# Half of the gates and branches by rows of tokens in a DeepNorm decoder trunk on one Trainium2 core

## The chip, the cores and the metric

The kernel runs on one core of a Trainium2 chip. The metric is the device time of one execution in microseconds (us), smaller is better. The core has five engines with a queue of instructions each: TensorE (PE; its weight loads are shown apart as PEld), VectorE (DVE), ScalarE (ACT), GpSimd (POOL) and SyncE (SP), which here does nothing but issue transfers. A queue is worked off in order: an instruction that waits holds up everything behind it on its engine.

## The reference

A decoder trunk of two layers over 256 tokens of width 1024, all in float32. Each layer is a half-step SwiGLU block, a mixer, and a second half-step SwiGLU block, each followed by a scaled residual and a layer norm. The change is in the mixer:

```python
    z = x @ w_in
    u, v, q, k, val, gates = jnp.split(z, SPLITS, axis=-1)
    ...
    h_a = _chunked_sgu(u, v, sgu_ln_g, sgu_ln_b, sgu_w, sgu_b)
    ...
    o = _diff_attention(q, k, val, lam_full)
    o = _rmsnorm(o, diff_ln_g) * (1.0 - lam_init)
    h_b = o.reshape(bsz, seq, DIFF_V_WIDTH)
    g = jax.nn.sigmoid(gates.reshape(bsz, seq, N_BRANCH, D_MODEL) + gate_b)
    m = g[:, :, 0] * (h_a @ w_branch[0]) + g[:, :, 1] * (h_b @ w_branch[1])
    return m @ w_out
```

So there are two gates of 1024 columns, each a product of the 256 x 1024 input with a 1024 x 1024 matrix and a bias; two branches, each again a product with a 1024 x 1024 matrix; the gated sum m; and the product of m with `w_out`.

## The kernel before, in words

**Numbers in two parts.** Every matrix product is made from float32 numbers split in a high part and a low remainder, both in a rounded float32 type. A product takes three passes: high by high, low weight by high input, high weight by low input. The weights come from memory as float32 and are split on the chip: `stream` (L150) issues a 1 MB load on SP into one of 4 `raw` buffers, ACT copies the high part into `whi` (L169) and DVE subtracts to give `wlo` (L171). One load gives two *pieces* of 128 x 1024 weights, and there are 8 buffers each for high and low pieces. An input in two parts lies with 256 high and 256 low values side by side, so that one matmul of 512 columns takes both.

**By columns of features.** `gemm_a2` (L243) holds a 128 x 128 block of weights in the array and streams tokens past it. For a block of 128 features it makes 8 wide matmuls of 512 columns (high weight by both parts of the input, L253) and 8 narrow ones of 256 columns (low weight by the high part, L260). The result stands with features on the partitions. It is evicted by ACT (one half, L261) and DVE (which adds the other, L263), four times for 512 features. The gates, `u`, `q`, `k` and both branches are made so.

**By rows of tokens.** `gemm_b` (L282) and `gemm_b2` (L302) hold a 128 x 128 block of the input (128 tokens) and stream 512 columns of weights; `rows_b` (L272) and `three` (L238) make three wide matmuls (L241) for each of the 8 values of k (blocks of 128 input features). The token halves t = 0 and t = 1 come one after the other. In `gemm_b` the last `tail` values of k are held back: their weights are used for all of t = 0 and then again for t = 1. In `gemm_b2`, which makes 1024 columns from two matrices of 512, all weights are. The result stands with tokens on the partitions, and one instruction evicts 512 columns.

**Order.** PE's order is written out in the code. Work that runs beside the big products is a generator handed to `beside` with a delay; `beat` counts PE's work in units and lets due generators emit their next instructions. A block of 128 features by columns counts 0.65 and 0.35, a piece of one token half by rows 0.5. The order on the other engines is made by the compiler's scheduler from priorities (program order) and readiness, and `behind(ins)` puts an instruction behind a given one of the same engine: `emptied` and `added` are the last eviction on ACT and DVE, `loaded` the last weight load on SP.

**A mixer's stages.** `val` (rows), then 8 times `q` or `k` (columns), each attended by a task beside; then gate A and gate B (columns, L727 to L736), `u` in part, `v` (rows), the rest of `u`, branch B from `hb` (the attention's output), branch A from `ha` (the spatial unit's output), the gated sum, and `w_out` (rows, L825). A branch (L804) is two calls of `gemm_a2` with two loads each; DVE multiplies a result with the gate (L808), and for branch A adds branch B's part (L815) and splits the sum into `mhi` and `mlo` (L206, L207), which stand with features on the partitions, as `w_out` needs them. In `w_out` the first half of k comes first for both token halves. Then comes the layer norm, whose result for t = 0 is turned by PE (L507) while t = 1 is still being made, and the next SwiGLU block, whose first weights are split into buffers that `w_out` gives back.

**Turning by transfer.** The SwiGLU block makes most of its hidden values by rows, and has to turn them: `parted` (L184) copies the 16-bit halves of the float32 numbers into two planes on POOL, `moved` (L188) is a transposing transfer on SP, `joined` (L192) puts the halves together again, and ACT and DVE split the result (L554, L556). This is the existing use of what the change does to the gated sum.

Of the kernel before, what the change touches and what calls it, by code (L numbers as in the profile page):

```python
# [20 lines left out]
P = 128  # L21
# [17 lines left out]
NEG = -1e30  # L39
ROPE_THETA = 10000.0  # L40
# [13 lines left out]
def trunk(ctx, tc, x, xT, w13a, w13b, w2, wb, wqk, wa, wbr, wo, gateb, sgug, sgub, sguwT, sgubias, lam, diffg,  # L54
# [247 lines left out]
    def gemm_b2(srcs, xh, xl, done, norm=None):  # L302
# [9 lines left out]
        for t in range(NT):  # L312
            for c in range(2):
                if norm:
                    norm.ready(t, c)
                    after[3] = [norm.xlo.get((0, 1))] * 2
                for m in range(2):
                    n = 2 * c + m
                    if t == 0:
                        got[m][2 * c : 2 * c + 2] = stream(srcs[m][:, c * CH : (c + 1) * CH], sub=512, lent=lent[n],  # L320
                                                           after=after[n])
                    for i in range(2 * c, 2 * c + 2):
                        rows_b(ps[t][m], t, 2 * i, got[m][i], xh, xl, KT)
            with behind(latest[0] if t == 0 else None):
                done(t, ps[t])
# [255 lines left out]
    def mixer(l, i, norm):  # L581
        xh, xl = parts(both)
        V_, VAL_ = 0, 1
        U_, GA_, GB_ = 0, 1, 2
# [137 lines left out]
        for hp in range(HEADS // 2):  # L722
            qT = rope(wqk[l, hp, 0], HD ** -0.5)
            kT = rope(wqk[l, hp, 1], 1.0)
            beside(attend(hp, qT, kT), 4.5 + 2.1 * hp)

        gates = []  # L727
        for br, sec in ((0, GA_), (1, GB_)):
            gt = slots("gate", KT)
            gates.append(gt)  # L730
            for c in range(KT // 2):
                (_, b), = gemm_a2([wa[l, sec, c]], both, lambda m: t512("gz"), lambda: t512("r"))
                for n in range(2):
                    s = slice(n * T, (n + 1) * T)
                    A.activation(gt[c][:, s], b[:, s], AF.Tanh, scale=0.5,
                                 bias=gbh[:, l, br, c * 2 + n : c * 2 + n + 1])  # L736
# [4 lines left out]
        def u_part(gps):  # L741
            for gp in gps:
                uu = slots("u", 2)[0]
                us.append(uu)
                (_, uu), = gemm_a2([wa[l, U_, gp]], both, lambda m: uu)
# [58 lines left out]
        def branch(br, h):  # L804
            for c in range(0, KT // 2, 2):
                for m, b in gemm_a2([wbr[l, br, c + m] for m in range(2)], lambda k: h[k], lambda m: t512("bz")):
                    g = gates[br][c + m]
                    V.scalar_tensor_tensor(out=g, in0=g, scalar=1.0, in1=b, op0=ALU.add, op1=ALU.mult)  # L808
                    yield c + m, g

        for _ in branch(1, hb):
# [13 lines left out]
        gemm_b2([wo[l, 0], wo[l, 1]], view(m_hi), view(m_lo), done)  # L825
# [3 lines left out]
    for l in range(DEPTH):  # L829
# [5 lines left out]
_INS = ["x", "xT", "w13a", "w13b", "w2", "wb", "wqk", "wa", "wbr", "wo", "gateb", "sgug", "sgub", "sguwT", "sgubias",  # L835
        "lam", "diffg", "lng", "lnb", "lngT", "lnbT", "cosT", "sinT"]


def _layout(i):
# [39 lines left out]
    o["wa"] = np.stack([pairs(w) for w in (u, ga, gb)], axis=1)  # L879
    o["wbr"] = pairs(f["w_branch"])  # L880
# [35 lines left out]
```

## Time and profile before

| | |
|---|---|
| median of 3 runs | 1220.32 us (1219.88 to 1220.91) |
| the profiled execution's own time | 1220.37 us |
| its span, first to last instruction | 1218.6 us |
| granted TensorE clock | 1.0 |

The profile is of one execution. The span is 1.8 us shorter than the time of the same execution, since the time holds what lies around the instructions. Times in the trace count from the span's start. A row of the chain of work gives the start, the duration, the engine with tile and line, and how many instructions were merged. A row of a group of instructions gives line, engine, operation, tiles (out<-in), shape, count, then busy us and mean ns of one, then idle time of the engine before them. In the trace's matmul rows the duration of a single matmul (about 390 ns for 512 columns) is longer than the distance to the next one, because matmuls overlap; the chain's durations divided by its counts give the distance.

### The profile page before, as it was taken

Reading aid. Unit: us, or ns where it says so; the run is one execution under the profiler, and the core shown is the slowest. Engines: PE = TensorE matmul, PEld = TensorE weight load, DVE = VectorE, ACT = ScalarE, POOL = GpSimd, SP = SyncE. Lnnn points to the kernel's source line nnn. Section 1 sums busy time; section 2 is a strip of 40 time slices with the busy share of each in tenths; the row PEclk is TensorE's granted clock in tenths of the full one; section 3 lists DMA queues with packets and bytes.
Section 4 is the critical chain, followed back from the end, with each engine's and each line's share of the span. In section 5 each row is a group of like instructions: output and inputs, shape, how many; then the busy total and the mean of one; then the engine's idle time right before and its main releaser. Section 6 shows DMA issues by size and latency. Waiting matters only on the chain.

```text
span 1218.6 us, 17027 instructions
## 1 busy us (share of the span) xinstructions
PE 1212.8 (100%) x6079; PEld 1025.6 (84%) x6079; DVE 887.9 (73%) x1516; ACT 716.0 (59%) x1372; POOL 283.1 (23%) x392
## 2 busy tenths in 40 slices
PE   9999999999999999999999999999999999999998
PEld 8888888888888888888888888888888888888887
DVE  6676667897688986766676756678875989676763
ACT  6465546669865555554455554466797664564740
POOL 1523100155320023230023330003544000323200
PEclk9999999999999999999999999999999999999999
DMA  9967645659564746867556757556675746667540
GB/s 343 328 196 240 242 173 178 242 192 274 194 214 144 250 157 211 246 203 259 190 164 204 250 194 259 205 183 221 215 206 189 250 155 226 189 224 243 178 185 35
DMA packets 103653, 257.55 MB, mean 211 GB/s; under 512 B 68320, under 2 KB 69392, under 8 KB 77456
## 3 DMA queue, kind: packets, MB, share of 16 engines
q1 hardware_dynamic: 99600, 243.82, 59.2%
q0 software_dynamic: 3536, 12.13, 3.3%
q8 instruction: 47, 0.77, 0.2%
q10 hardware_dynamic: 432, 0.52, 0.1%
q14 instruction: 38, 0.31, 0.1%
HBM read 235.47 MB, written 1.05 MB: 194 GB/s over the span
## 4 chain that ended last, share of the span: by engine, by line
PE 99%; DMA 0%; DVE 0%; ACT 0%; issue 0%; ACTq 0%
PE bank L241 64%; PE bank L253 19%; PE bank L260 10%; PE bank L356 2%; PE sbank L629 1%; PE sbank L507 1%; PE sbank L685 1%; PE sbank L786 1%; DMA xraw<-in_xT 0%; PE sbank L683 0%; PE sbank L479 0%; DVE xtok L487 0%; ACT whi L206 0%; DVE st L452 0%; DVE xtok L448 0%; ACT x L206 0%
## 5 line engine op out<-in xcount | busy, mean ns | idle before, releaser
L171 DVE TENSOR_TENSOR wlo<-raw,whi 128x512 fp32r<-128x512 f32 (+1 forms) x570 | 524.1, 954 | 133.1 <-ACT whi L169 87.7
L169 ACT ACTIVATE whi<-raw 128x512 fp32r<-128x512 f32 (+1 forms) x570 | 432.7, 799 | 234.3 <-PE bank L241 158.3
L241 PE MATMUL bank<-whi,x 128*128 128x512 f32 x1352 | 421.8, 390 | 0.0
L241 PEld LDWEIGHTS bank<-whi,x 128*128 128x128 f32 x1352 | 253.9, 188 | 52.6
L241 PE MATMUL bank<-wlo,x 128*128 128x512 f32 x676 | 263.1, 389 | 0.0
L253 PE MATMUL bank<-x,whi 128*128 128x512 f32 x768 | 183.9, 391 | 0.0
L253 PEld LDWEIGHTS bank<-x,whi 128*128 128x128 f32 x768 | 141.5, 188 | 28.1
L184 POOL COPY planes<-planes 128x512 uint16<-128x512 uint16 x80 | 83.3, 1068 | 321.2 <-DVE planes L539 321.2
L241 PEld LDWEIGHTS bank<-wlo,x 128*128 128x128 f32 x676 | 127.0, 188 | 25.7
L241 PE MATMUL bank<-whi,hhi 128*128 128x512 f32 (+1 forms) x374 | 141.2, 378 | 0.0
L241 PE MATMUL bank<-wlo,hhi 128*128 128x512 f32 (+1 forms) x374 | 141.0, 377 | 0.0
L241 PE MATMUL bank<-whi,hlo 128*128 128x512 f32 (+1 forms) x374 | 140.8, 377 | 0.0
L260 PEld LDWEIGHTS bank<-x,wlo 128*128 128x128 f32 x768 | 97.9, 191 | 3.6
L260 PE MATMUL bank<-x,wlo 128*128 128x256 f32 x768 | 100.4, 284 | 0.0
L192 POOL COPY planes<-planes 128x512 uint16<-128x512 uint16 x80 | 70.5, 925 | 91.7 <-DMA planes<-planes 91.4
L539 DVE TENSOR_TENSOR planes<-planes,bank 128x512 f32<-128x512 f32 x40 | 27.3, 683 | 86.4 <-issue 70.8
L538 ACT ACTIVATE planes<-bank 128x512 f32<-128x512 f32 x40 | 24.0, 599 | 102.8 <-PE bank L241 101.8
L605 POOL TENSOR_TENSOR swap<-swap,sin_t 128x512 f32<-128x512 f32 x16 | 29.5, 1843 | 235.0 <-DMA swap<-z 202.6
L241 PEld LDWEIGHTS bank<-whi,hlo 128*128 128x128 f32 x374 | 70.4, 188 | 13.1
L241 PEld LDWEIGHTS bank<-whi,hhi 128*128 128x128 f32 x374 | 70.4, 188 | 12.8
L241 PEld LDWEIGHTS bank<-wlo,hhi 128*128 128x128 f32 x374 | 70.4, 188 | 12.5
L261 ACT ACTIVATE r<-bank 128x256 f32<-128x256 f32 x128 | 46.5, 372 | 25.6 <-PE bank L260 25.6
(179 smaller groups left out, 1288.2 us busy)
## 6 DMA issues: line engine op xcount, KB each, us to landing
raw<-in_w13b SPq DMA_DIRECT2D x76, 1024.0 KB, 5.4
raw<-in_w SPq DMA_DIRECT2D x40, 1024.0 KB, 6.0
raw<-in_wa SPq DMA_DIRECT2D x24, 1024.0 KB, 5.1
raw<-in_wb SPq DMA_DIRECT2D x16, 1024.0 KB, 5.0
raw<-in_wqk SPq DMA_DIRECT2D x16, 1024.0 KB, 4.8
raw<-in_wbr SPq DMA_DIRECT2D x16, 1024.0 KB, 5.0
raw<-in_w13a SPq DMA_DIRECT2D x8, 1024.0 KB, 5.1
raw<-in_wo SPq DMA_DIRECT2D x8, 1024.0 KB, 4.9
```

What stands on the lines that cost most here:

```text
L169: A.activation(h, r, AF.Copy)
L171: V.tensor_tensor(out=w, in0=r, in1=h.bitcast(F32), op=ALU.subtract)
L184: G.tensor_copy(out=planes(out)[:, w], in_=numbers(src)[:, w])
L192: eng.tensor_copy(out=numbers(out)[:, w], in_=planes(src)[:, w])
L241: PE.matmul(ps, xx, w, start=start and n == 0, stop=stop and n == 2)
L253: PE.matmul(b[-1], hi[:, k * P : (k + 1) * P], xc(k), start=k == 0, stop=False)
L260: PE.matmul(b[n][:, :T], lo[:, k * P : (k + 1) * P], xc(k)[:, :T], start=False, stop=k == KT - 1)
L261: emptied[0] = A.activation(r[:, s], b[n][:, T:], AF.Copy, scale=scale).ins
L356: PE.matmul(ps[t][m], x[:, j, o + t * P : o + (t + 1) * P], y, start=k0 + j == 0 and o == 0 and y is hi, stop=k0 + j == KT - 1 and y is lo)
L538: silu[0] = A.activation(s, ps[0], AF.Silu).ins
L539: added[0] = V.tensor_tensor(out=s, in0=s, in1=ps[1], op=ALU.mult).ins
L605: turned_by[0] = G.tensor_tensor(out=s3, in0=s3, in1=s, op=ALU.mult).ins
```

## The change

For the gates and for the branches, the first 512 of the 1024 columns are made by rows of tokens (`gemm_b`, with everything held back: `TAIL` is 8), the other 512 by columns as before. For each of the two, the order is now: gate A rows, gate A columns, gate B rows, gate B columns; branch B rows, branch B columns, branch A rows, branch A columns. The weights are laid out accordingly on the host (`wgr`, `wbrr` for rows).

A gate's rows need their bias along the columns: 1024 values are broadcast to all partitions by a POOL transfer of 512 KB (`gbias`, after the second pair of heads), and DVE adds them on eviction before ACT's tanh.

A branch's rows are multiplied with the gate by one DVE instruction for each token half. For branch A, DVE adds branch B's part, and the sum of 128 tokens by 512 features is turned by a task beside (`turned`): parted (t = 0 by POOL alone, t = 1 by ACT and POOL, one plane each), moved by one transposing transfer, joined by POOL, split by ACT and DVE into the first two tiles of `mhi` and `mlo`. That makes two such transfers in each layer. In `w_out`, t = 1 takes the second half of k first (`second=(1, 0)`).

```diff
-    def rows_b(ps, t, k0, piece, xh, xl, kts, c0=0, n=512):
+    def rows_b(ps, t, k0, piece, xh, xl, kts, c0=0, n=512, first=0):
...
-                  k == 0, k == kts - 1)
+                  k == first, k == (first - 1) % kts)
...
-    def gemm_b2(srcs, xh, xl, done, norm=None):
+    def gemm_b2(srcs, xh, xl, done, norm=None, second=(0, 1)):
...
         for t in range(NT):
-            for c in range(2):
+            order = second if t else (0, 1)
+            for c in order:
...
             beside(attend(hp, qT, kT), 4.5 + 2.1 * hp)
-
-        gates = []
-        for br, sec in ((0, GA_), (1, GB_)):
-            gt = slots("gate", KT)
+            if hp == 1:
+                gbias = bc_load(gatebr[l], qT[:, :1])
+
+        gates, grow = [], []
+
+        def gate_rows(br):
+
+            gr = [slots("gr", 2)[0] for _ in range(NT)]
+            grow.append(gr)
+
+            def done(t, ps, c, n):
+                added[0] = V.tensor_tensor(out=gr[t], in0=ps, in1=gbias[:, br * 512 : (br + 1) * 512], op=ALU.add).ins
+                emptied[0] = A.activation(gr[t], gr[t], AF.Tanh, scale=0.5).ins
+
+            gemm_b(wgr[l, br, 0], KT, xh, xl, done, tail=TAIL)
+
+        def gate_columns(br):
+            gt = slots("gate", KT // 2)
             gates.append(gt)
-            for c in range(KT // 2):
-                (_, b), = gemm_a2([wa[l, sec, c]], both, lambda m: t512("gz"), lambda: t512("r"))
+            for c in range(KT // 4):
+                (_, b), = gemm_a2([wg[l, br, c]], both, lambda m: t512("gz"), lambda: t512("r"))
...
+        for br in range(2):
+            gate_rows(br)
+            gate_columns(br)
...
+        def branch_rows(br, h):
+            def done(t, ps, c, n):
+                g = grow[br][t]
+                a = V.scalar_tensor_tensor(out=g, in0=g, scalar=1.0, in1=ps, op0=ALU.add, op1=ALU.mult)
+                if br == 0:
+                    a = V.tensor_tensor(out=g, in0=g, in1=grow[1][t], op=ALU.add)
+                    beside(turned(t, g, grow[1][t]), 0)
+                added[0] = a.ins
+
+            gemm_b(wbrr[l, br, 0], KT, lambda k: h[k][:, :T], lambda k: h[k][:, T:], done, tail=8)
+
+        def turned(t, g, p):
+            if t == 0:
+                parted(g, p)
+            else:
+                A.activation(planes(p)[:, 0], numbers(g)[:, 0], AF.Copy)
+                G.tensor_copy(out=planes(p)[:, 1], in_=numbers(g)[:, 1])
+            yield (3.2, 4.6)[t]
+            with behind(loaded[0]):
+                moved(p, g)
+            yield 0.1
+            joined(g, p, G)
+            yield (0.5, 1.4)[t]
+            for j in range(2):
+                hi, lo = (v[j].rearrange("p (k t) -> p k t", k=2)[:, :, t * P : (t + 1) * P] for v in (m_hi, m_lo))
+                f = p.rearrange("p (k t) -> p k t", k=4)[:, 2 * j : 2 * j + 2]
+                with behind(settled[0] if t else emptied[0]):
+                    A.activation(hi, f, AF.Copy)
+                with behind(settled[1] if t else added[0]):
+                    V.tensor_tensor(out=lo, in0=f, in1=hi.bitcast(F32), op=ALU.subtract)
+
+        def branch_columns(br, h):
+            for c, b in gemm_a2([wbr[l, br, m] for m in range(2)], lambda k: h[k], lambda m: t512("bz")):
+                g = gates[br][c]
+                V.scalar_tensor_tensor(out=g, in0=g, scalar=1.0, in1=b, op0=ALU.add, op1=ALU.mult)
+                yield c, g
+
+        branch_rows(1, hb)
+        for _ in branch_columns(1, hb):
             pass
-        m_hi, m_lo = slots("mhi", KT, F32R), slots("mlo", KT, F32R)
-        for c, m in branch(0, ha):
+        m_hi += slots("mhi", KT, F32R)
+        m_lo += slots("mlo", KT, F32R)
+        branch_rows(0, ha)
+        for c, m in branch_columns(0, ha):
             V.tensor_tensor(out=m, in0=m, in1=gates[1][c], op=ALU.add)
-            split(m_hi[c], m_lo[c], m)
+            settled = split(m_hi[KT // 4 + c], m_lo[KT // 4 + c], m)
...
-        gemm_b2([wo[l, 0], wo[l, 1]], view(m_hi), view(m_lo), done)
+        gemm_b2([wo[l, 0], wo[l, 1]], view(m_hi), view(m_lo), done, second=(1, 0))
```

More of the change, by code (lines that the diff above doesn't have):

```diff
@@ L39 @@
 NEG = -1e30
+TAIL = 8
 ROPE_THETA = 10000.0
@@ L802, in mixer @@
         u_part((2, 3))
[L804 to L811, printed above, removed]
-            pass
-        m_hi, m_lo = slots("mhi", KT, F32R), slots("mlo", KT, F32R)
@@ L878, in _layout @@
     o["wqk"] = np.stack([pairs(w) for w in (q, k)], axis=2)
-    o["wa"] = np.stack([pairs(w) for w in (u, ga, gb)], axis=1)
-    o["wbr"] = pairs(f["w_branch"])
+    o["wu"] = pairs(u)
+    o["wg"] = np.stack([pairs(w[..., 512:]) for w in (ga, gb)], axis=1)
+    o["wgr"] = np.stack([halves(w[..., :512]) for w in (ga, gb)], axis=1)
+    o["wbr"] = pairs(f["w_branch"][..., 512:])
+    o["wbrr"] = halves(f["w_branch"][..., :512])
+    o["gatebr"] = c(f["gate_b"].reshape(L, 2, D)[..., :512]).reshape(L, D)
     o["wo"] = halves(f["w_out"])
```

17 lines of the change are left out of this document (8 added, 9 removed).

## The prediction

> **What bounds the kernel now.** I read the page first: busy shares, granted clock, and the chain that ended last.
>
> ```profile
> PE 1212.8 (100%) x6079; PEld 1025.6 (84%) x6079; DVE 887.9 (73%) x1516; ACT 716.0 (59%) x1372; POOL 283.1 (23%) x392
> ...
> PEclk9999999999999999999999999999999999999999
> ...
> PE 99%; DMA 0%; DVE 0%; ACT 0%; issue 0%; ACTq 0%
> ```
>
> PE is busy all the span, the clock is granted in full, and 99% of the chain is PE's own matmuls following one another. So time can be won in two ways only: cheaper matmuls, or the few short waits between them. It can be lost wherever PE starts to wait. Next I read the chain in order of time, for the distance between matmuls (start, us, count). L253 is the wide matmul by columns, L260 the narrow one, L241 the wide one by rows.
>
> ```profile
> 277.38 3.65 PE bank L253 x16
> 281.04 1.91 PE bank L260 x16
> 282.95 3.65 PE bank L253 x16
> ...
> 354.99 7.72 PE bank L253 x32
> ...
> 381.24 7.53 PE bank L253 x32
> 388.77 3.83 PE bank L260 x32
> 392.61 7.28 PE bank L253 x32
> ...
> 403.72 17.71 PE bank L241 x78
> ...
> 426.44 6.85 PE bank L241 x30
> ...
> 437.11 99.31 PE bank L241 x438
> ...
> 958.25 7.28 PE bank L253 x32
> ...
> 984.07 7.55 PE bank L253 x32
> ```
>
> Wide matmuls follow at 227 ns (99.31 / 438, 17.71 / 78), narrow ones at 120 ns (3.83 / 32), not at half of 227. The wide matmuls that open a branch take 7.72 and 7.53 us in the first layer, 7.28 and 7.55 in the second; those inside a branch (392.61) take 7.28. The waits of the weight loads for 340 to 450 us name what they waited for:
>
> ```profile
> PEld bank L253 <- DVE u L263: 0.3, 1, 0.3
> PEld bank L253 <- DVE ha L207: 0.3, 1, 0.3
> PEld bank L253 <- DVE hb L719: 0.2, 1, 0.2
> ```
>
> A branch by columns touches all eight blocks of `hb` or `ha` within its first 1.8 us (8 x 227 ns), and the last block is late.
>
> **The change, part by part.** *PE.* A unit is 512 columns for 256 tokens and 1024 features. By columns that is 32 wide and 32 narrow matmuls: 2 x (282.95 - 277.38) = 11.14 us in the gates, 403.72 - 392.61 = 11.11 us in the branches. By rows it is 2 x 8 x 3 = 48 wide ones: 48 x 226.9 ns = 10.89 us. Four gate units over two layers save 4 x 0.25 = 1.0 us, four branch units 4 x 0.22 = 0.9 us: **1.9 us**. The number of streamed columns is the same (48 x 512); what goes is the part of a narrow matmul above half of a wide one.
>
> [...]
>
> *The waits on `hb` and `ha`.* By rows, t = 0 goes through k in pairs, 6 matmuls (1.36 us) each, and reaches the last pair 4.1 us after its start; the waits above are 0.2 to 0.3 us long. They go, and so does the one on the eviction of `u`, since two accumulators are opened at once and stand free two products earlier. Worth (7.72 - 7.28) + (7.53 - 7.28) + (7.55 - 7.28) = **0.96 us**. What is next late there: nothing that the view of waits names.
>
> *Evictions.*
>
> ```profile
> L261 ACT ACTIVATE r<-bank 128x256 f32<-128x256 f32 x128 | 46.5, 372 | 25.6 <-PE bank L260 25.6
> L735 ACT ACTIVATE gate<-gz,gbh 128x256 f32<-128x256 f32 x32 | 15.5, 503 | 7.1 <-DVE gz L263 7.1
> L263 DVE TENSOR_TENSOR bz<-bank,r 128x256 f32<-128x256 f32 x32 | 13.0, 418 | 0.0
> L808 DVE SCALAR_TENSOR_TENSOR gate<-gate,bz 128x512 f32<-128x512 f32 x16 | 11.0, 685 | 0.0
> L207 DVE TENSOR_TENSOR mlo<-gate,mhi 128x512 fp32r<-128x512 f32 x8 | 5.5, 685 | 0.0
> ```
>
> ```profile
> L184 POOL COPY planes<-planes x80: 609/945/5167, 25.9 to 1143.9; 128x512 uint16<-128x512 uint16 x80
> L192 POOL COPY planes<-planes x80: 757/770/1753, 38.0 to 1149.3; 128x512 uint16<-128x512 uint16 x80
> L554 ACT ACTIVATE hhi<-planes x80: 397/407/413, 49.4 to 1157.2; 128x256 fp32r<-128x256 f32 x80
> L556 DVE TENSOR_TENSOR hlo<-planes,hhi x80: 405/418/961, 53.9 to 1160.1; 128x256 fp32r<-128x256 f32 x80
> L538 ACT ACTIVATE planes<-bank x40: 582/599/604, 24.4 to 1136.6; 128x512 f32<-128x512 f32 x40
> ...
> DMA to landing us min/median/max: 2.7/5.9/9.6
> ```
>
> The second fence is the SwiGLU block's turned tile, the nearest thing to the new one (ns min/median/max). A gate unit costs ACT 4 x 372 + 4 x 503 = 3.5 us now and 2 x 599 = 1.2 after; DVE 4 x 418 = 1.7 now, 2 x 685 = 1.4 after. A branch unit saves ACT 4 x 372 = 1.5 us and DVE 4 x 418 = 1.7. The split of the turned half takes DVE 4 x 418 = 1.7 in place of 2 x 685 = 1.4. Per layer DVE has some 3.6 us less and ACT some 6 less; neither bounds, so this is worth nothing by itself. It is cover for what is added.
>
> *Bursts.* With everything held back, t = 0 takes a piece of weights each 1.36 us, twice the pace of columns. This costs nothing as long as splits stand ready:
>
> ```profile
> ACT whi L169 <- PE bank L241: 158.3, 142, 9.4
> ```
>
> ACT's largest wait is for PE to give back a weight buffer, so the eight buffers are mostly full and a unit needs four. Bound: 0 to 0.3 us a unit, the size of a single wait above; I take 0.
>
> *The turned half.* The window of the branches and the end of the last product by columns:
>
> ```profile
> 354.80:403.50 48.70, 48.70 (x290) 42.66 (x289) 43.31 (x81) 29.23 (x54) 0.00 (x0) 1.00 0.52 179
> ```
>
> ```profile
> 401.84 0.38 ACT L261 ACTIVATE r<-bank 128x256 f32<-128x256 f32 x1 [0.49 <-PE bank L260]
> ```
>
> POOL is idle there (0.00), DVE busy for 43.3 of 48.7 us. For t = 0 PE goes on for 24 x 0.227 = 5.45 us with t = 1 and 11.11 us with the columns: `w_out` asks for the turned half 16.6 us later. The chain: two DVE instructions 1.37, parting 2 x 0.945 = 1.9, transfer 5.9, joining 2 x 0.77 = 1.5, together 10.7 us. Its split is placed behind the second narrow eviction, which before starts 1.9 us ahead of `w_out` (403.72 - 401.84) and so at 14.7: 4.0 us of slack. The split itself (0.38 for that eviction, then 0.41, 0.42) ends its first pair near 15.9 and its second 0.4 later; the first low part is asked for at 16.6 + 2 x 0.23 = 17.0, the second 1.36 later. Cost 0. For t = 1 the order of k gives 16.3 us (10.89 + 5.45) after the start of `w_out`, and its chain is over before 403.72. Without cover the chain would cost its whole 12 us a layer.
>
> *SP.*
>
> ```profile
> 366.85 20.97 SPq L156 DMA_DIRECT2D raw<-in_wo  x4
> 394.92 29.41 SPq L156 DMA_DIRECT2D raw<-in_w13b  x7
> ```
>
> The transfer of t = 0 is due at 403.7 - 16.6 + 1.4 + 1.9 = 390.4, between the last `w_out` load (ended at 387.8) and the next block's first (394.92): free. If it is placed early, it holds loads whose weights are first used at 426.44, the next block's start; if it is placed behind the load at 394.92, it is 4.5 us late, about the slack. Cost 0 to 1 us a layer, I take 0.
>
> *Two new instructions in front of the last split.*
>
> ```profile
> 409.56 0.69 DVE L207 TENSOR_TENSOR mlo<-gate,mhi 128x512 fp32r<-128x512 f32 x1
> ```
>
> ```profile
> 410.84 0.39 PE L241 MATMUL bank<-whi,mlo 128*128 128x512 f32 x1
> ```
>
> The last `mlo` ends 0.6 us before PE's first use of it. Two instructions of 0.42 us stand ahead of it now. DVE's queue held weight splits there that are wanted later, so they take those places; bounds 0 to 0.3 us a layer (0.84 - 0.59), I take 0.
>
> *Buffers.* With the halves of k exchanged, `w_out` gives its first buffers back 4 x 1.36 = 5.45 us later:
>
> ```profile
> 416.09 1.16 ACT L169 ACTIVATE whi<-raw 128x512 fp32r<-128x512 f32 x2 [3.98 <-PE bank L241]
> ```
>
> These splits move to 421.5. They are used near 430 (the fourth piece from 426.44), so 7 us remain, but they now fall beside the turning of the norm. Bounds 0 to 1.2 us a layer, one pair of them; I take 0.
>
> *The bias.* One 512 KB broadcast a layer, on POOL's queue, landing in about 4.5 us and asked for 30 us later: 0.
>
> ```profile
> bc<-in_sgug POOLq DMA_DIRECT2D x2, 512.0 KB, 4.5
> ```
>
> **Sum:** 1.9 + 0.96 = 2.85 us off the profiled execution's 1220.37: **1217.5 us**. The median of the runs shown, 1220.32, is 0.05 from it.
>
> **Rivals.** *A short wait at the merge:* chain, split or buffers lose 0.3 to 1.4 us a layer; against it stands the slack, for it DVE's 89% there. Middle 0.8 x 2 gives 1219.1, at most 1220.3.
>
> *Slower: POOL's copies starve.* The longest parting copy stands beside six of DVE's weight splits in a row:
>
> ```profile
> 451.42 3.69 DVE L171 TENSOR_TENSOR wlo<-raw,whi 128x512 fp32r<-128x512 f32 x6
> ```
>
> ```profile
> 451.56 5.72 POOL L184 COPY planes<-planes 128x512 uint16<-128x512 uint16 x2 [6.02 <-DVE planes L539]
> ```
>
> While `w_out`'s weights are split at one piece each 1.36 us, DVE is as dense. With all maxima the chain takes 1.37 + 5.8 + 9.6 + 3.5 = 20.3 us, its split ends at 21.5, and PE waits 4.5 us a layer: 1217.5 + 9 = 1226.5. It eats the whole gain from 1.4 us a layer on, which is 5.5 us more than the chain's 10.7; one maximum alone (3.8 or 3.7) is not enough. Against it: the medians are taken beside the same splits. [...]
>
> *Nothing from the pitch:* if matmuls cost by their columns alone, rows and columns cost the same, 0.96 us remain, 1219.4. The 120 ns speak against it.
>
> **How the numbers follow.** The forecast 0.50; the short wait 0.30; slower 0.15; nothing from the pitch 0.05. A measurement can tell about 0.2%, 2.4 us: the bound is 1217.9, only 0.4 under which the forecast lies, so it gives 0.42 of its 0.50 to faster; with 0.01 of the short wait, 0.43. Slower 0.14 (0.01 of that rival stays within), the same 0.43. The range runs from 1217.0 (half a us more of waits found) to 1222.7, which leaves out about 0.03 below and 0.14 above.
>
> **What would show it.** 128 matmuls fewer; none at 120 ns but the columns' half; the chain still 99% PE; no wait of the weight loads on `hb`, `ha` or `u`. Right after the last narrow matmul of branch A, no wait on the split of the turned half; POOL's joining over before the second narrow eviction. Wrong would be: `w_out`'s first weight load waiting on that split or on POOL, DVE splits late in the next block, or rows at more than 227 ns.

## The result and the profile after

The changed kernel takes 1230.5 us (median of 6 runs, 1229.78 to 1231.39) against 1220.19 us (6 runs, 1219.88 to 1220.91): a ratio of 1.0084, 95% interval 1.0071 to 1.0097. It is **slower by 10.3 us**; the forecast was 1217.5. The profiled execution took 1231.39 us, its span is 1229.7 us. From the branch of the gates on, the lines of the changed file lie up to 53 further down; the ones used below are L172 (weight split on DVE), L242 (matmul by rows), L254 and L261 (wide and narrow by columns), L630 (the attention's scores), L684 (its product with the values), L738 and L739 (a gate row's addition on DVE and tanh on ACT).

The page of the changed kernel, busy times, clock and the chain that ended last:

```profile
PE 1214.1 (99%) x5951; PEld 1020.0 (83%) x5951; DVE 886.2 (72%) x1498; ACT 704.1 (57%) x1338; POOL 306.5 (25%) x408
...
PEclk9999999999999999999999999999999999999999
...
PE 58%; DVE 7%; ACT 6%; DMA 3%; POOL 2%; issue 2%; SPq 0%; DVEq 0%; POOLq 0%; ACTq 0%
```

There are 6079 - 5951 = 128 matmuls fewer, as forecast, and the clock is still granted in full. But the chain is no longer PE's alone: its share fell from 99% to 58%. DVE and ACT are busy for less time than before (886.2 against 887.9, 704.1 against 716.0). So the loss can't be work that was added; it has to be waiting. The chain of the changed kernel between 340 and 430 us gives the distances between matmuls (start, us, count):

```profile
349.12 3.63 PE bank L254 x16
352.75 1.91 PE bank L261 x16
...
385.83 10.91 PE bank L242 x48
```

A unit by rows takes 10.91 us, as forecast (10.89). One by columns takes 2 x (3.63 + 1.91) = 11.08 here, a little less than the forecast's 11.14, so a gate unit by rows gains 0.17 us and not 0.25. Next the first mixer by stages, before and then after: from the first score to the first matmul of branch B, the two branches, and `w_out` to the next block (window, its length, then busy time and count of PE, PEld, DVE, ACT, POOL, then clock, DMA share, GB/s).

```profile
233.49:354.82 121.33, 121.33 (x713) 105.83 (x713) 94.31 (x206) 96.70 (x238) 54.11 (x97) 1.00 0.67 212
354.82:403.56 48.74, 48.74 (x291) 42.70 (x289) 43.35 (x81) 29.21 (x54) 0.00 (x0) 1.00 0.52 179
403.56:426.20 22.64, 22.64 (x107) 18.72 (x105) 21.41 (x45) 12.46 (x24) 1.08 (x2) 1.00 0.71 247
```

```profile
233.74:360.07 126.33, 122.44 (x682) 104.47 (x682) 93.38 (x203) 92.80 (x225) 57.84 (x98) 1.00 0.69 209
360.07:407.66 47.59, 47.59 (x258) 41.27 (x257) 41.15 (x70) 26.97 (x48) 4.87 (x6) 1.00 0.62 195
407.66:430.50 22.84, 22.82 (x106) 18.64 (x105) 22.55 (x48) 12.85 (x26) 3.20 (x4) 1.00 0.62 213
```

The stage in which the gates are made beside the attention is 5.00 us longer, in a stage that was to become 0.5 us shorter. The branches are 1.15 us shorter, `w_out` 0.20 us longer. In the second layer the three differences are +5.91, -0.72 and +0.71. Together +10.91, -1.87 and +0.91; 1.15 us more are spread over the rest of the span. What PE's weight loads waited for, in the whole run of the changed kernel (us in total, times, longest):

```profile
PEld sbank L684 <- POOL onT L185: 3.9, 2, 1.9
PEld sbank L630 <- ACT sbank L694: 3.7, 4, 1.9
PEld sbank L684 <- POOL aT L185: 3.3, 2, 1.7
PEld sbank L630 <- issue: 2.8, 8, 0.4
PEld sbank L509 <- DVE xtok L465: 2.5, 4, 0.7
```

The waits on `hb`, `ha` and `u` are gone. In their place stand three waits of the attention, 3.9 + 3.7 + 3.3 = 10.9 us, as much as that stage lost; none of them appears in the run before. At L684 the view names POOL's parting, but the operand that L684 reads is made by ACT, which joins the 16-bit halves of the probabilities (L678), and the rows of the matmuls themselves name that:

```profile
PE sbank L684 <- ACT d L678: 5.6, 4, 1.5
```

The wait for the norm's `xtok` grew from 0.8 to 2.5.

**Two mechanisms in the trace.** First, the eviction of a gate row. DVE of the changed kernel near 270 us (start, us, line, tiles; idle time before it in brackets), then ACT, then PE:

```profile
268.49 5.36 DVE L172 TENSOR_TENSOR wlo<-raw,whi 128x1024 fp32r<-128x1024 f32 x4
273.77 0.68 DVE L738 TENSOR_TENSOR gr<-bank,bc 128x512 f32<-128x512 f32 x1
```

```profile
274.48 0.63 ACT L739 ACTIVATE gr<-gr 128x512 f32<-128x512 f32 x1 [1.50 <-DVE gr L738]
275.01 0.26 ACT L694 ACTIVATE sbank<-sbank 128x128 f32<-128x128 f32 x1
```

```profile
275.44 0.71 PE L630 MATMUL sbank<-qk,qk 64*128 64x128 f32 x6 [0.57 <-ACT sbank L694]
```

A row unit uses up its four pieces at once, so four weight splits stand together in DVE's queue, and the row's addition behind them. ACT's next instruction is the tanh, which needs that addition; behind the tanh stands the attention's last sum of squares (L694), and PE's scores wait for the bank that it reads. Half of a softmax then starts later. ACT itself stands idle for the row additions four times in the run, and what is behind the tanh in its queue starts later for it:

```profile
ACT gr L739 <- DVE gr L738: 7.9, 4, 2.4
```

Second, the broadcasts for the spatial unit's norm (`sgug`, `sgub`) are tied to the first gate column. It now comes after the rows of gate A: the first broadcast is issued at 286.51 us (272.2 before), the second, which also waits for the buffer of the gates' bias, at 303.80 (272.8 before). There the attention's transposing transfers are under way. Transfers issued between 284 and 300 us, before and then after (queue, count, KB, us to landing):

```profile
on<-onT SPq DMA_TRANSPOSE x1, 4.6
...
d<-aT SPq DMA_TRANSPOSE x1, 6.2
```

```profile
bc<-in_sgug POOLq DMA_DIRECT2D x1, 512.0 KB, 5.1
...
on<-onT SPq DMA_TRANSPOSE x1, 8.3
d<-aT SPq DMA_TRANSPOSE x1, 7.6
```

DVE had the joining of the first of these (`on<-onT`) next in its queue and stood for it; ACT stood for DVE's softmax, and joined the probabilities 12.5 us after they had landed (298.2):

```profile
297.46 0.80 DVE L193 COPY onT<-on 128x512 uint16<-128x512 uint16 x2 [7.43 <-DMA on<-onT]
```

```profile
300.87 0.51 ACT L644 ACTIVATE pp<-pp,mx 128x256 f32<-128x256 f32 x1 [5.94 <-DVE mx L642]
...
310.67 1.41 ACT L678 ACTIVATE aT<-d 128x512 uint16<-128x512 uint16 x2
```

PE's weight loads stand for them from 311.6 to 313.3. Which of the two mechanisms costs how much, the runs had to tell.

### The profile page after: what moved, and what is told of

The parts are those of the page before. It is cut to its first block, busy times and chain, and to the rows that moved or that the text cites. A ratio compares the mean times of both kernels' runs of the same rounds, so it can differ in the third digit from the quotient of the medians.

```text
span 1229.7 us, 16740 instructions
## 1 busy us (share of the span) xinstructions
PE 1214.1 (99%) x5951; PEld 1020.0 (83%) x5951; DVE 886.2 (72%) x1498; ACT 704.1 (57%) x1338; POOL 306.5 (25%) x408
## 4 chain that ended last, share of the span: by engine, by line
PE 58%; DVE 7%; ACT 6%; DMA 3%; POOL 2%; issue 2%; SPq 0%; DVEq 0%; POOLq 0%; ACTq 0%
PE bank L242 48%; PE bank L254 6%; DVE wlo L172 3%; PE bank L261 2%; ACT whi L170 2%; DMA on<-onT 1%; ACT pp L644 1%; DMA swap<-z 1%; ACT aT L678 1%; PE sbank L804 1%; POOL swap L606 1%; ACT on L703 1%; DVE llo L172 1%; PE sbank L509 0%; DMA raw<-in_wu 0%
## 5 line engine op out<-in xcount | busy, mean ns | idle before, releaser
L172 DVE TENSOR_TENSOR wlo<-raw,whi 128x512 fp32r<-128x512 f32 (+1 forms) x570 | 524.3, 958 | 128.2 <-ACT whi L170 90.5
L242 PE MATMUL bank<-whi,x 128*128 128x512 f32 x1480 | 462.6, 390 | 0.0
L242 PEld LDWEIGHTS bank<-whi,x 128*128 128x128 f32 x1480 | 277.9, 188 | 57.4
L242 PE MATMUL bank<-wlo,x 128*128 128x512 f32 x740 | 288.1, 389 | 0.0
L242 PEld LDWEIGHTS bank<-wlo,x 128*128 128x128 f32 x740 | 139.0, 188 | 28.2
L254 PE MATMUL bank<-x,whi 128*128 128x512 f32 x640 | 153.7, 392 | 0.2 <-DVE gz L264 0.2
L242 PE MATMUL bank<-whi,hhi 128*128 128x512 f32 (+1 forms) x374 | 141.2, 378 | 0.0
L242 PE MATMUL bank<-wlo,hhi 128*128 128x512 f32 (+1 forms) x374 | 141.0, 377 | 0.0
L242 PE MATMUL bank<-whi,hlo 128*128 128x512 f32 (+1 forms) x374 | 140.9, 377 | 0.0
L254 PEld LDWEIGHTS bank<-x,whi 128*128 128x128 f32 x640 | 118.0, 188 | 24.1 <-DVE gz L264 0.4
L261 PEld LDWEIGHTS bank<-x,wlo 128*128 128x128 f32 x640 | 81.4, 191 | 2.9
L261 PE MATMUL bank<-x,wlo 128*128 128x256 f32 x640 | 82.6, 283 | 0.0
L242 PEld LDWEIGHTS bank<-whi,hlo 128*128 128x128 f32 x374 | 70.4, 188 | 12.9
L242 PEld LDWEIGHTS bank<-whi,hhi 128*128 128x128 f32 x374 | 70.4, 188 | 12.8
L242 PEld LDWEIGHTS bank<-wlo,hhi 128*128 128x128 f32 x374 | 70.4, 188 | 12.8
L515 ACT ACTIVATE xf<-sbank,ln_b,ln_g 128x128 f32<-128x128 f32 x80 | 30.1, 457 | 41.2 <-PE sbank L509 41.2
```

Of the source, the lines that this page charges most:

```text
L172: V.tensor_tensor(out=w, in0=r, in1=h.bitcast(F32), op=ALU.subtract)
L242: PE.matmul(ps, xx, w, start=start and n == 0, stop=stop and n == 2)
L254: PE.matmul(b[-1], hi[:, k * P : (k + 1) * P], xc(k), start=k == 0, stop=False)
L261: PE.matmul(b[n][:, :T], lo[:, k * P : (k + 1) * P], xc(k)[:, :T], start=False, stop=k == KT - 1)
L515: A.activation(xf[:, s], b[:, s], AF.Identity, scale=self.gT[:, f], bias=self.bT[:, f])
```

## The experiments

In the texts on record, A is at first the theory that the loss lies in the gates, where PE waits for the attention, and not in the merge behind branch A; from the columns-first run on, A is the broadcasts' part of it and B the row evictions. The table has each kernel's stages from its trace (first layer / second layer, us) and its median. "Before" and "after" are the two kernels of this study. The stages are those of one profiled execution, which lies up to 1.4 us from its kernel's median (after: 0.9 above; broadcasts late: 1.3 below).

| kernel | gates | branches | `w_out` | median |
|---|---|---|---|---|
| before | 121.33 / 121.17 | 48.74 / 48.31 | 22.64 / 22.64 | 1220.2 |
| after | 126.33 / 127.08 | 47.59 / 47.59 | 22.84 / 23.35 | 1230.5 |
| branches alone | 121.15 / 121.46 | 47.60 / 47.59 | 23.40 / 23.37 | 1220.3 |
| gates alone | 125.33 / 125.22 | 50.01 / 48.92 | 22.64 / 22.64 | 1230.4 |
| join on POOL | 127.46 / 127.08 | 47.59 / 47.59 | 22.86 / 23.36 | 1231.7 |
| broadcasts late | 123.87 / 124.04 | 47.59 / 47.60 | 22.84 / 23.36 | 1226.9 |
| columns first | 122.20 / 121.50 | 47.59 / 47.60 | 23.36 / 23.19 | 1220.5 |
| no gate bias | 123.14 / 122.62 | 47.60 / 47.60 | 22.88 / 23.36 | 1223.0 |
| default order | 125.84 / 126.52 | 47.59 / 47.60 | 22.88 / 22.86 | 1230.6 |
| other addend | 126.78 / 125.77 | 47.59 / 47.59 | 22.85 / 22.89 | 1230.3 |
| late, no bias | 121.53 / 121.52 | 47.59 / 47.60 | 22.88 / 23.40 | 1220.0 |
| columns first, default order | 121.82 / 121.41 | 47.59 / 47.59 | 23.35 / 23.40 | 1221.2 |
| 4 held back | 125.35 / 126.22 | 47.60 / 47.60 | 22.84 / 23.36 | 1229.4 |
| one load | 122.28 / 121.71 | 47.62 / 47.83 | 23.40 / 23.19 | 1221.1 |
| one load, default order | 121.61 / 121.79 | 47.62 / 47.62 | 23.38 / 23.37 | 1219.9 |
| split early, default order | 121.47 / 122.21 | 47.61 / 47.62 | 22.64 / 22.64 | 1219.2 |
| split early | 121.48 / 122.15 | 47.62 / 47.62 | 22.63 / 22.64 | 1219.0 |

### Which half of the change

*The branches alone by rows:*

```diff
-        for br in range(2):
-            gate_rows(br)
-            gate_columns(br)
+        for br in range(2):
+            gt = slots("gate", KT)
...
+            grow.append(gt[: KT // 4])
+            gates.append(gt[KT // 4 :])
```

> The branches by rows with the turned half and the exchanged order in w_out stay; the gates are made by columns again, and the branches' rows are multiplied with a gate tile that stands by features, so the numbers of the gated sum are not the reference's. Theory A (the loss sits in the stage of the gates by rows, where PE comes to wait for the attention): the two branch stages keep their 1.9 us, the norm loses up to 0.9, 1218.5 to 1219.5 us. Rival (the turning of the gated sum or its buffers cost the time): 1228 or more.

Measured: 1220.32 us, ratio 1.0002 (0.999 to 1.0013). The rival is out: the merge and the turning transfer don't cost the 10 us. But the gain is missing too, and the time lies 0.8 us above A's range. The branches are 1.86 us shorter in sum, as after the whole change (1.87), and the stretch from `w_out` to the next block is 0.76 + 0.73 = 1.49 us longer.

*The gates alone by rows* (branches by columns, nothing turned):

```diff
-        branch_rows(1, hb)
-        for _ in branch_columns(1, hb):
+        for _ in branch(1, hb):
...
-        gemm_b2([wo[l, 0], wo[l, 1]], view(m_hi), view(m_lo), done, second=(1, 0))
+        gemm_b2([wo[l, 0], wo[l, 1]], view(m_hi), view(m_lo), done)
```

> The gates by rows stay; both branches are made by columns, with no transposing transfer of the gated sum and the old order in w_out; the row gates are used as if they stood by features, so the gated sum is not the reference's. Theory A: the loss stays and the branches' gain goes, 1230.5 + 1.9 - 0.9 = about 1231.5 us. Rival (the merge): 1219 to 1220.

Measured: 1230.44 us, ratio 1.0087 (1.0057 to 1.0116). The loss sits in the gates. Here a part of it shows behind the stage, in branch B, which by columns touches the attention's `hb` at once and waits for it.

### Which mechanism in the gates

*The attention's output joined by POOL and not by DVE*, so that DVE does not stand for the transfer:

```diff
-            with behind(added[0]):
-                joined(on, onT, V)
+            joined(on, onT, G)
```

> The changed kernel with one edit: the attention's output is joined by POOL and not by DVE, so that DVE does not stand in its queue for the transfer. Theory A in its narrow form (DVE's wait of 7.4 us in each layer for that transfer makes the next heads' softmax late, and PE waits for those): DVE's wait is gone and with it at least the PE waits of 1.4 and 1.7 us in each layer, 1222 to 1225 us. Rival (the heads are late for another reason: the broadcasts that now run beside the transfers, or ACT's order): no change beyond 1 us, 1229.5 to 1231.5.

Measured: 1231.71 us, ratio 1.0097 (1.0068 to 1.0126). A miss. DVE's stand of 7.4 us is gone, and so is PE's wait at 311.6. But POOL now stands for the transfers in DVE's place (7.3 and 9.4 us for the first two), with the steps of the attention's norm behind it in its queue, and ACT waits for these (5.4 us in the changed kernel from 262 to 345 us):

```profile
ACT on L703 <- POOL nwy L235: 8.0, 3, 3.8
```

PE's longest wait at L684 grew from 1.9 to 3.5 us. The edit moved the stand to another engine, so it doesn't tell what the stand itself costs.

*The two broadcasts of the spatial unit behind the first half of `u`:*

```diff
-        g_bc, b_bc = (bc_load(v[l], gates[0][0][:, :1]) for v in (sgug, sgub))
         us = []
...
         u_part((0, 1))
+        g_bc, b_bc = (bc_load(v[l], us[1][:, :1]) for v in (sgug, sgub))
```

> The changed kernel with one edit: the two broadcasts for the spatial unit's norm are issued after the first half of u and not after the gates, so that they no longer run beside the attention's transposing transfers (one of which took 8.3 us to land beside a broadcast, 4.6 at the same place before). If the collision makes the transfers late: DVE's wait shrinks by about 4 us and the time falls to 1223 to 1227 us. Theory A in its narrow form (the wait stands where it stands because the join was queued too early, whatever the transfer takes): it falls by at most 2 us, 1228.5 or more.

Measured: 1226.86 us, ratio 1.0051 (1.0029 to 1.0074): 3.6 us come back. The same transfer lands in 5.5 us:

```profile
on<-onT SPq DMA_TRANSPOSE x1, 5.5
d<-aT SPq DMA_TRANSPOSE x1, 5.8
```

So the broadcasts are a cause, but by the medians a third of it. PE's wait for L694 is still there (3.3 us in that run).

*The columns of both gates ahead of the rows of both:*

```diff
-        for br in range(2):
-            gate_rows(br)
-            gate_columns(br)
+        for br in range(2):
+            gate_columns(br)
+        for br in range(2):
+            gate_rows(br)
```

> The changed kernel with the columns of both gates ahead of the rows of both. Theory A (the loss comes from the two broadcasts for the spatial unit's norm, which hang on the first gate column and which the rows ahead of it push in among the attention's transposing transfers): the first broadcast is asked for some 11 us earlier again, at about 275 us; the second still waits until the bias of the gates gives its buffer back, behind the last gate row. So about half of what the late broadcasts gave back: 1227 to 1229.5. Rival B (the loss comes from the row evictions, a DVE addition and a tanh behind it, in whose queues the attention's operations stand): the evictions only move, 1229.5 to 1232.

Measured: 1220.48 us, ratio 1.0002 (0.9991 to 1.0014): all of the 10 us, more than either theory by itself allowed. This order undoes both at once. The first broadcast is issued at 273.8 again, and the row evictions fall at 290 to 313 us, among other neighbours. ACT still stands for two of the eight row additions (4.5 us in the run), but PE now waits only 1.5 us for what is behind them (L694). PE's waits of that run:

```profile
PEld sbank L630 <- issue: 2.8, 8, 0.4
PEld sbank L509 <- DVE xtok L465: 2.8, 4, 0.7
PEld sbank L630 <- ACT sbank L694: 1.5, 2, 1.0
```

Both waits at L684 are gone (0.2 us remain). A third buffer for the broadcasts, meant to let the second one leave early too, did not fit into the on-chip memory (14 KB per partition were needed where 11.5 were left), so that variant has no time. To separate the mechanisms, the next run left the order alone.

*No bias for the gate rows:* no broadcast, no addition, ACT's tanh from PSUM.

```diff
-            if hp == 1:
-                gbias = bc_load(gatebr[l], qT[:, :1])
...
-                added[0] = V.tensor_tensor(out=gr[t], in0=ps, in1=gbias[...], op=ALU.add).ins
-                emptied[0] = A.activation(gr[t], gr[t], AF.Tanh, scale=0.5).ins
+                emptied[0] = A.activation(gr[t], ps, AF.Tanh, scale=0.5).ins
```

> The changed kernel without the bias of the gate rows: no broadcast for it, no addition on DVE, and ACT takes the tanh straight from PSUM. The first half of the gates lacks its bias. Theory A: both broadcasts for the spatial unit's norm are now asked for together at about 286 us, still among the transfers, 1228.5 to 1231. Rival B: the wait of ACT's tanh for DVE's addition goes with its queue, 1224 to 1227.

Measured: 1223.03 us, ratio 1.0026 (1.0015 to 1.0038): 7.5 us come back, as B has it and more than it allowed for. The broadcasts are still among the transfers, which are still slow (7.1 and 7.4 us):

```profile
267.69 5.43 DVE L172 TENSOR_TENSOR wlo<-raw,whi 128x1024 fp32r<-128x1024 f32 x4
274.39 0.42 DVE L642 CUSTOM_DVE_ANT_0 pp<-sbank,mask 128x256 f32<-128x256 f32 x1 [1.27 <-PE sbank L630]
```

These are the same four splits as in the changed kernel, but nothing behind them keeps ACT; DVE now waits for PE and not the other way round. ACT's next two joinings of probabilities start at 281.96 and 307.18 us, in the changed kernel at 284.29 and 310.67. The run took two things away, though: the addition and the broadcast of the bias with its buffer.

*The addition kept, with a table that is on the chip anyway in place of the bias:*

```diff
-                added[0] = V.tensor_tensor(out=gr[t], in0=ps, in1=gbias[...], op=ALU.add).ins
+                added[0] = V.tensor_tensor(out=gr[t]..., in0=ps..., in1=cos_t..., op=ALU.add).ins
...
-                gbias = bc_load(gatebr[l], qT[:, :1])
```

> The changed kernel, but DVE adds a table that is on the chip anyway (the cosines) in place of the gates' bias, so the addition with the tanh behind it stays and only the broadcast of the bias and its buffer go. The first half of the gates gets a wrong addend. It splits what the run without a bias took away together. If the addition in DVE's queue is what costs: 1228 to 1231, as the changed kernel. If the broadcast, or the buffer for which the second one of the spatial unit waits, costs: 1222 to 1224.5, as without a bias.

Measured: 1230.26 us, ratio 1.008 (1.0062 to 1.0099). The bias's broadcast and buffer cost nothing that can be measured; the addition with the tanh behind it does, although it takes DVE 0.68 us eight times, 5.4 us in a span in which DVE is idle for 343.

*Both repairs, no bias and late broadcasts:*

```diff
-            if hp == 1:
-                gbias = bc_load(gatebr[l], qT[:, :1])
...
-                added[0] = V.tensor_tensor(out=gr[t], in0=ps, in1=gbias[...], op=ALU.add).ins
-                emptied[0] = A.activation(gr[t], gr[t], AF.Tanh, scale=0.5).ins
+                emptied[0] = A.activation(gr[t], ps, AF.Tanh, scale=0.5).ins
...
-        g_bc, b_bc = (bc_load(v[l], gates[0][0][:, :1]) for v in (sgug, sgub))
...
+        g_bc, b_bc = (bc_load(v[l], us[1][:, :1]) for v in (sgug, sgub))
```

> Without the gates' bias and with the spatial unit's broadcasts late: both repairs at once (the first half of the gates lacks its bias). If the evictions' chain (7.5 us) and the broadcasts beside the transfers (3.6 us) are two causes that add up, nearly all of the 10.3 us comes back: 1219 to 1221. If both repairs hit the same wait: 1222.5 to 1224.

Measured: 1220.04 us, ratio 0.9998 (0.9987 to 1.0008). By the medians 7.5 and 3.6 us come back apart and 10.5 together, but the 3.6 rests on three runs (1225.5 to 1227.0), and the traces show that the causes overlap: the gates' stages of the two layers are together 7.65 us shorter without the bias, 5.50 with late broadcasts and 10.36 with both. Of PE's three waits, the 3.3 us at L684 go with either repair, so they need both causes. Without the bias 3.1 of the other 3.9 us at L684 stay, and 1.0 of the 3.7 for L694; with late broadcasts 2.3 and 3.3. With both repairs the gates' stage is back at 121.5 us. It isn't shorter than before by the 0.5 us a layer that the pitch gives.

*Half of the values of k held back in the gate rows instead of all:*

```diff
-TAIL = 8
+TAIL = 4
```

> The changed kernel with 4 of 8 values of k held back in the gate rows in place of all, so that the weight buffers come free in steps and the splits don't stand four in a row ahead of the second row addition. If that burst makes the addition late: 1225 to 1229. If the addition stands in the way by its own place in the queue: 1229.5 to 1231.5.

Measured: 1229.41 us, ratio 1.0073 (1.0055 to 1.0092), just under the second case's range. The place of the wait changed: both waits at L684 are gone, and the wait of the scores for L694 rose from 3.7 to 6.6 us, ACT's stand for the row additions from 7.9 to 14.3. Spreading the splits didn't help here, where the pair of addition and tanh still stood ahead of the attention's work.

### Where the branches' gain went

*`w_out`'s order of k the same in both halves again:*

```diff
-        gemm_b2([wo[l, 0], wo[l, 1]], view(m_hi), view(m_lo), done, second=(1, 0))
+        gemm_b2([wo[l, 0], wo[l, 1]], view(m_hi), view(m_lo), done)
```

> The changed kernel with w_out's order of k the same in both halves of the tokens, as before. If the later return of w_out's buffers is what the norm's turning pays for, the stretch from w_out to the next block falls from 22.84 and 23.35 us to the 22.64 of the kernel before: 1229.3 to 1230.2. Rival: the turned half of the second tokens is now asked for 5.4 us earlier and is late: the same stretch grows by 0.5 to 1.5 us, 1231 to 1233.5.

Measured: 1230.58 us, ratio 1.0082 (1.0052 to 1.0111). Neither case: the stretch is 22.88 and 22.86. With the exchanged order it was 22.85 and 22.89 in the run with another addend, so the order of k is not what decides. The same edit on top of columns first:

> The columns of both gates ahead of the rows of both, and w_out's order of k the same in both halves of the tokens. If the later return of w_out's buffers costs 0.5 us a layer at the norm: 1219.3 to 1220.0, against 1220.5 with the exchanged order. Rival: no difference, 1220.3 to 1220.8.

Measured: 1221.22 us, ratio 1.0005 (0.9996 to 1.0014), and the stretch is 23.35 and 23.40. The rival holds, though the time lies 0.4 us above its range: the exchanged order and the later return of `w_out`'s buffers are not the cause. DVE of that run shows another one, ahead of `w_out` (which starts at 403.32):

```profile
395.62 0.68 DVE L172 TENSOR_TENSOR wlo<-raw,whi 128x512 fp32r<-128x512 f32 x1
400.70 0.69 DVE L172 TENSOR_TENSOR wlo<-raw,whi 128x512 fp32r<-128x512 f32 x1 [4.39 <-issue]
...
421.12 1.00 DVE L465 TENSOR_SCALAR xtok<-xtok,mv,nwy 128x512 f32<-128x512 f32 x2
```

DVE stands for 4.4 us at a weight split, and then works without a pause (17.5 of the 17.8 us from 403.32) until it writes the norm's `xtok` at 421.12, 17.80 us after `w_out`'s start; before, that instruction came 15.8 us after it (419.36 and 403.56). The four pieces that the rows gave back are refilled by then, and the columns of a branch, one call with two loads, do 32 wide matmuls before the first narrow one, whose end gives a low buffer back. To test that, a branch's columns were made in two calls, on top of columns first, once with the exchanged and once with the default order of k:

```diff
-            for c, b in gemm_a2([wbr[l, br, m] for m in range(2)], lambda k: h[k], lambda m: t512("bz")):
+            for c in range(2):
+                (_, b), = gemm_a2([wbr[l, br, c]], lambda k: h[k], lambda m: t512("bz"))
```

> The columns of both gates ahead of the rows, and the columns of a branch in two steps of one load each in place of one step with two, so that the narrow matmuls, which give the low weight buffers back, come after 16 wide ones and not after 32. Theory: DVE's stand of 4.4 us at a weight split in branch A is for a low buffer, and the backlog that it leaves makes the norm late; then the stand falls to some 2 us, the stretch from w_out to the next block from 23.2 and 23.4 us to 22.6 or 22.8, and the time to 1218.8 to 1219.8. Rival: DVE's stand is for something else, and the norm is late because DVE has more to do in w_out: the stretch stays at 23.2 to 23.4, the time at 1220.2 to 1221.

> As the run before it, with w_out's order of k the same in both halves of the tokens. Theory: the same gain, 1218.8 to 1219.8, if the order of k doesn't matter; with the low buffers free earlier, the turned half of the second tokens could become the late one, then 1220.5 to 1222.

Measured: 1221.14 us, ratio 1.0006 (0.9997 to 1.0014), and 1219.89 us, 0.9995 (0.9985 to 1.0004). The first run's DVE row and two of its waits:

```profile
396.92 0.69 DVE L172 TENSOR_TENSOR wlo<-raw,whi 128x512 fp32r<-128x512 f32 x1 [1.48 <-issue]
```

```profile
PEld bank L242 <- DVE mlo L854: 1.9, 4, 0.8
...
PEld sbank L509 <- DVE xtok L465: 0.7, 2, 0.3
```

The theory of the stand holds and the time does not follow (the first run lies above both its ranges, the second just above the theory's): the stand fell from 4.4 to 1.5 us and the norm's wait from 2.8 to 0.7, but the stretch stays at 23.40 and 23.19, because PE now waits 1.9 us for the split of the turned half (L854), which the new spacing of the calls had put later. Moving that split two beats ahead was the last edit, in the default order of k and in the exchanged one:

```diff
-            yield (3.2, 4.6)[t]
+            yield (2.7, 4.6)[t]
...
-            yield (0.5, 1.4)[t]
+            yield (0.1, 1.4)[t]
```

> Columns of the gates first, branches' columns in steps of one load, w_out's order of k the same in both halves, and now the split of the turned half of the first tokens two beats earlier, behind the second narrow eviction of branch A's first step (its data are joined by then). The waits of PE for that split (2.0 us in the run before, 4 times) should go without the one for the norm coming back: the stretch from w_out to the next block falls from 23.4 to 22.8 us or less in both layers, the time to 1218.5 to 1219.3. Rival: DVE has no room, and the wait moves to the norm again or to another split: 1219.7 to 1220.5.

> The same with the exchanged order of k in w_out: 1218.5 to 1219.5 if that order doesn't matter, as found so far.

Measured: 1219.17 us, ratio 0.9991 (0.9983 to 1.0), and **1218.97 us, ratio 0.9988 (0.9979 to 0.9998)**. The stretch behind `w_out` in the second of them, both layers:

```profile
402.12:424.75 22.63, 22.63 (x106) 18.72 (x105) 19.97 (x42) 12.43 (x25) 2.80 (x4) 1.00 0.72 252
1005.20:1027.84 22.64, 22.64 (x106) 18.72 (x105) 20.38 (x42) 12.44 (x25) 2.98 (x4) 1.00 0.71 251
```

It is back at 22.63 and 22.64 us, with the branches at 47.62: their gain is kept. This version, the change with the gates' columns first, a branch's columns in steps of one load and the earlier split, is faster than both kernels, by about 0.1% against the one before; the interval only just excludes no difference, and it is the best of several versions measured.

## Why the prediction was wrong, point by point

- **The step that failed is "Evictions"**, and its sentence "neither bounds, so this is worth nothing by itself. It is cover for what is added". The busy times in it are right: a tanh took 0.63 and an addition 0.68. What it left out is the order in the queues. By columns, an eviction's steps were short and stood between single weight splits; a gate row has two long steps, DVE first and ACT behind it, in the middle of the attention that shares both queues. ACT stands 7.9 us for DVE in that pair, and without it 7.2 to 7.5 us come back (against another addend, against the changed kernel), a part of them shared with the broadcasts. The saving for DVE was also too large: 3.6 us a layer were forecast, and its busy time fell by 1.7 in the whole run.
- **"The bias"** was rightly costed at 0 for its own broadcast (another addend: 1230.3). But the sentence stopped there. The two broadcasts that were there already hang on the first gate column, and the rows go ahead of it; the step moved them 14 and 31 us, into the transposing transfers, 3.6 us by the medians. This is a moved step whose transfers I did not count.
- **PE's pitch** was right by rows (10.91 us a unit) and a little too large by columns in the gates (11.08, so 0.7 us in place of 1.0 for the four gate units). In the branches it and **the waits on `hb` and `ha`** give 1.87 us together, the 0.9 + 0.96 of the forecast. In the gates the gain never shows: in the best runs that stage still has 0.15 to 1.0 us a layer more than before. Part of it are the waits for L694 that stay (1.5 us in all); the rest is open.
- **"Bursts"**: as a price on PE, 0 was right, no wait on a weight buffer appeared. The burst is still part of the failure: it puts four splits in front of the row's addition. By itself it is not the cause (4 held back: 1229.4 us).
- **The turned half, SP and the merge** cost nothing that can be measured in the changed kernel, as forecast; POOL's copies of the tile took 0.6 to 1.3 us each, and the rival that lets them starve did not come.
- **"Buffers"** had the right size (0 to 1.2 us a layer; measured 0.2 and 0.7, and 0.75 with the branches alone) and the wrong reason: not the order of k in `w_out`, but low buffers held by the columns until their narrow matmuls. Taking 0 was a mistake, since the profile showed DVE at 43.3 of 48.7 us there: PE got ahead by 0.9 us a layer, and DVE, which now stood 4.4 to 4.6 us for a low buffer, had no room to follow.
- **The rivals** for a loss all sat behind the gates. None was about the longest stage that the change touches, in which the attention runs beside it, and so the range ended at 1222.7.

## What to carry to other kernels

When work is moved into a stage that has a second chain beside it, read that stage's queues instruction by instruction: here an eviction of two engines in a row cost 7.2 to 7.5 us by what stood behind its second half, where its additions were busy for 5.4 us on an engine that was idle for 343. List everything that is tied to a result whose place moves, broadcasts and buffers too, and see what it lands among. A gain on PE in a stretch where DVE has no slack can turn up as the next wait: with the branches alone, 1.86 us won in them came back as 1.49 us behind them, where DVE was busy for 17.29 of the first 17.85 us of the first layer's `w_out`. Here the gain was kept only when the buffers came back earlier and a split was moved as well (22.63 and 22.64 us).

## What the runs showed of the hardware

The time of one transposing transfer of 128 x 512 float32 numbers (256 KB) ran from 3.0 to 8.3 us in one stage of the two kernels. The transfers of the attention's output (`on<-onT`) from 262 to 345 us, shortest, median and longest, four in the kernel before and then three in the changed one:

```profile
DMA to landing us min/median/max: 3.5/4.8/7.4
```

```profile
DMA to landing us min/median/max: 3.0/7.4/8.3
```

From issue to landing, 256 KB in 3.0 us are 87 GB/s, in 8.3 us 32 GB/s. For one of them a neighbour was tried: with the broadcasts moved away, the transfer of 8.3 us took 5.5.

POOL's two copies of a joining took 1.89 us in one run and 3.71 in another, with DVE's instructions beside them, whose addition took 1.20 us in the first and 0.68 in the second. The joining of the turned half and DVE beside it, first in the run with columns first and default order, then in the run with one load:

```profile
393.32 1.89 POOL L193 COPY gr<-gr 128x512 uint16<-128x512 uint16 x2 [3.14 <-DMA gr<-gr]
```

```profile
393.66 0.92 DVE L172 TENSOR_TENSOR wlo<-raw,whi 128x512 fp32r<-128x512 f32 x1
394.50 1.20 DVE L830 TENSOR_TENSOR gr<-gr,gr 128x512 f32<-128x512 f32 x1
```

```profile
392.36 3.71 POOL L193 COPY gr<-gr 128x512 uint16<-128x512 uint16 x2 [2.87 <-DMA gr<-gr]
```

```profile
393.56 0.68 DVE L172 TENSOR_TENSOR wlo<-raw,whi 128x512 fp32r<-128x512 f32 x1
394.16 0.68 DVE L830 TENSOR_TENSOR gr<-gr,gr 128x512 f32<-128x512 f32 x1
```

In the first, POOL's two copies take 1.89 us and DVE's split and addition 0.92 and 1.20; in the second, DVE keeps its 0.68 and POOL needs 3.71. Whether either is the cause of the other, and what decides which of them is the longer, was not tried.
